# Model dimension counted as 512 a + 4 p + j, expert weights in 8 KB pieces, output weights and weighted sums stored block by block

## The chip, the cores and the metric

The kernel runs on one core of a Trainium2 chip. The metric is the device time of one execution in microseconds (us); lower is better. The engines are called as in the profile: PE (TensorE matmuls), PEld (its weight loads, which overlap the matmuls), DVE (VectorE), ACT (ScalarE), POOL (GpSimd), SP (the queue that issues nearly all loads from HBM).

## The reference

Two layers of a decoder trunk on one sequence of 256 tokens with 1024 features, all in float32. Layer 0 mixes by a causal convolution and stick-breaking attention, layer 1 by gated linear attention and causal pooling; both end with the same mixture of 16 experts, and these carry most of the bytes.

```python
for l in range(DEPTH):                                   # 2
    sh1, sc1, g1, sh2, sc2, g2 = split(silu(c) @ ada_w[l] + ada_b[l], 6)
    h = rmsnorm(x, norm_mix[l]) * (1 + sc1) + sh1
    x = x + g1 * mixer_l(h, w_in, w_out, ...)            # ends in  concat @ w_out
    h = rmsnorm(x, norm_ffn[l]) * (1 + sc2) + sh2
    # 16 experts in 4 groups, top 2 of one group per token
    for e in range(16):
        y += combine[:, e:e+1] * ((silu(h @ w_gate[l, e]) * (h @ w_up[l, e])) @ w_down[l, e])
    x = x + g2 * y
return rmsnorm(x, final_norm)
```

Gate, up and down of one expert are 1024 x 512, 1024 x 512 and 512 x 1024 float32, 2 MB each: 192 MB for both layers.

## The kernel before

**Layout.** The 1024 features lie on 128 partitions in 8 blocks. Feature 256 a + 2 p + j (a below 4, j below 2) is in block 2 a + j on partition p (`rows`, `block`, L72 to L79). A matrix that is contracted over the features is loaded with `rows`, so each partition reads two neighbouring rows. A vector along the features is cut into blocks by `block`, every second element of a run of 256.

**Weights.** All weights pass through one ring of 16 buffers of 1 MB (`buffer`, L50). SP issues their loads in a fixed order, each as soon as the buffer 16 places earlier was read for the last time. `unit` (L62) loads a piece of ada_w (the conditioning products), w_in or w_out; a piece of w_in is two transfers of 512 KB.

**Projections and output products.** `Projections` (w_in) and `Output` (w_out) split each 128 x 512 piece of weight into a high part (ACT, L55) and a low part (DVE, sometimes POOL, L56), and PE multiplies in three passes (L418, L423 and L453). For w_out the weight is PE's stationary operand, and `products` (L453) takes it by `block`, at a step of two elements.

**Experts (`moe`).** Experts are worked in 8 pairs. The two experts of a pair use the two halves of PE's columns. For a pair, `weight` (L1215) loads 12 units of 1 MB: 4 of gate, 4 of up, 4 of down. A unit holds one quarter of the contraction for both experts, so a partition reads 4 KB of each expert. `up` (L1240) takes a unit for every two blocks: 4 matmuls, which the profile shows as 8 records. `act` and `actT` multiply with the SiLU and turn the 512 features onto partitions. `down` (L1277) does the down product, a unit for each of 4 blocks, two halves of 512 columns each. `evicted` and `high_low` (L1305, L1313) weight the result and split it into a high and a low part, and `scatter` (L1330) adds it into the four accumulators: in layer 0 with the parts as stationary operand, taken by `block`; in layer 1 as moving operand. The last pair of layer 0 uses `weighted_parts` (L1321) instead. Ahead of pair 7 stands a branch (`rest`, L1383) that is for experts with more than 64 tokens. In layer 1 the residual is added by 16 transposes that write the accumulators by `block` (L1538).

**Order.** It is written out by hand: pair n + 1's gate and up stand before pair n's down, and what fills the mixers (ada units, splits) is placed by generators.

```python
def rows(w):
    return w.rearrange("(a p j) n -> p a j n", a=4, j=2)
def block(ap, k):
    a, j = k // 2, k % 2
    return ap[:, 256 * a + j:256 * a + 256:2]
```

## Time and profile before

| what | value |
|---|---|
| runs | 791.4, 794.8 and 4035.95 us, median 794.8 |
| profiled execution | 791.18 us |
| its span in the profile | 789.5 us |
| PE busy, share of the span | 730.9 us, 93% |
| loads | 282.46 MB, mean 358 GB/s |
| stages by the timeline | mixer 0 to about 200 us, experts of layer 0 to 425, mixer 1 to 561, experts of layer 1 to 784 |

The profile is of one execution. The span is what its instructions cover; 1.7 us of the execution's own time lie around it. A busy PE is not a PE at its peak, since a matmul's row runs on while the next has begun; so stops and distances between starts say more than busy shares.

### The profile page before, as it was taken

What the parts mean: (1) busy time and instruction counts of PE and PEld (TensorE: products, weight loads), DVE (VectorE), ACT (ScalarE), POOL (GpSimd) and SP (SyncE); (2) the same over time, 40 slices, a digit from 0 to 9 for tenths busy, and PEclk for the clock granted to TensorE, in tenths of its full rate; (3) what the DMA queues carried; (4) which work ended last, traced back from release to release, by engine and by line L of the source; (5) the groups of instructions that cost most, each with busy time, mean ns of one, the idle gap of its engine ahead of it and who ended that gap; (6) DMA issues with size and microseconds to landing.
All of it is one profiled execution on the core that took longest, in us unless ns stands there. A gap on an engine that the chain in (4) does not pass through costs nothing. (4 is left out here: it accounts for less than half of the span.)

```text
span 789.5 us, 10674 instructions
## 1 busy us (share of the span) xinstructions
PE 730.9 (93%) x4173; PEld 402.8 (51%) x4173; DVE 313.8 (40%) x563; ACT 235.1 (30%) x441; POOL 120.0 (15%) x168
## 2 busy tenths in 40 slices
PE   6798888998899999999797999999999999999985
PEld 4398645486434335343233677579534334434323
DVE  3459968675214113121115655453513123213214
ACT  3357657463102101110113544551402101001012
POOL 1357646222000000000004500010300000000000
PEclk9999999999999999999999999999799999999999
DMA  8999739954999999999999998496699999999992
GB/s 357 386 375 419 291 121 398 372 219 183 351 410 409 409 409 409 409 408 409 409 405 391 396 414 322 171 402 235 255 385 412 408 409 409 409 408 409 408 403 106
DMA packets 74713, 282.46 MB, mean 358 GB/s; under 512 B 5194, under 2 KB 6438, under 8 KB 69530
## 3 DMA queue, kind: packets, MB, share of 16 engines
q1 hardware_dynamic: 73122, 278.68, 89.9%
q0 software_dynamic: 1344, 2.64, 0.9%
q8 instruction: 35, 0.57, 0.3%
q10 hardware_dynamic: 184, 0.34, 0.1%
q14 instruction: 28, 0.23, 0.1%
HBM read 280.59 MB, written 1.05 MB: 357 GB/s over the span
## 5 line engine op out<-in xcount | busy, mean ns | idle before, releaser
L1252 PE MATMUL g<-w,xg 128*64 128x512 f32 x512 | 115.0, 597 | 1.9 <-DMA w<-in_moe_w_gate_dram 1.8
L1252 PE MATMUL u<-w,xg 128*64 128x512 f32 x496 | 110.7, 594 | 2.1 <-DMA w<-in_moe_w_up_dram 2.1
L1285 PE MATMUL dn<-w,at 128*64 128x512 f32 x448 | 101.7, 604 | 8.1 <-ACTq L1383 6.8
L1264 DVE TENSOR_TENSOR act<-sg,u 128x512 f32<-128x512 f32 (+1 forms) x18 | 11.1, 628 | 153.0 <-PE u L1252 153.0
L1252 PEld LDWEIGHTS u<-w,xg 128*64 128x64 f32 x496 | 34.6, 137 | 72.1 <-issue 64.7
L1252 PEld LDWEIGHTS g<-w,xg 128*64 128x64 f32 x512 | 35.1, 137 | 68.6 <-issue 61.2
L56 DVE TENSOR_TENSOR g<-wi,g 128x512 fp32r<-128x512 f32 x72 | 58.1, 816 | 24.8 <-ACT g L55 24.6
L1285 PEld LDWEIGHTS dn<-w,at 128*64 128x64 f32 x448 | 31.1, 138 | 70.8 <-issue 56.8
L423 PE MATMUL pj<-hT,g 128*128 128x256 f32 x480 | 61.4, 285 | 6.0 <-DVE g L56 4.7
L423 PEld LDWEIGHTS pj<-hT,g 128*128 128x128 f32 x480 | 57.8, 188 | 10.0 <-DVE g L56 6.8
L418 PE MATMUL pj<-g,hT 128*128 128x512 f32 x192 | 51.3, 414 | 7.4 <-DVE g L56 3.5
L55 ACT ACTIVATE g<-wi 128x512 fp32r<-128x512 f32 x72 | 44.4, 626 | 39.1 <-PE pj L423 20.2
L190 PE MATMUL ada<-ad,cond 128*32 128x512 f32 x384 | 52.0, 653 | 4.0 <-DMA ad<-in_ada_w_dram 4.0
L453 PE MATMUL po<-cat,g 128*128 128x256 f32 x372 | 51.1, 290 | 2.5 <-ACT gsr L1006 1.7
L453 PEld LDWEIGHTS po<-cat,g 128*128 128x128 f32 x372 | 46.8, 196 | 6.7 <-ACT gsr L1006 2.6
L418 PEld LDWEIGHTS pj<-g,hT 128*128 128x128 f32 x192 | 35.4, 193 | 22.4 <-DVE g L56 6.7
L568 POOL TENSOR_TENSOR yc<-yc,cv 128x256 f32<-128x256 f32 x45 | 38.9, 864 | 22.8 <-ACT cv L567 20.0
L553 DVE SCALAR_TENSOR_TENSOR yc<-yp,epar,yc 128x256 f32<-128x256 f32 x56 | 41.3, 737 | 1.0
L1317 ACT ACTIVATE ys<-y 128x512 fp32r<-128x512 f32 x28 | 16.9, 625 | 67.1 <-DVE y L1307 62.3
L1275 DVE COPY at<-at 128x512 f32<-128x512 f32 x14 | 9.7, 692 | 67.5 <-PE at L1274 65.9
L1311 ACT ACTIVATE y<-dn,cw 128x512 f32<-128x512 f32 x7 | 4.8, 687 | 103.8 <-PE dn L1285 103.8
L1260 ACT ACTIVATE sg<-g 128x512 f32<-128x512 f32 x14 | 8.4, 597 | 89.4 <-PE g L1252 89.4
(385 smaller groups left out, 887.4 us busy)
## 6 DMA issues: line engine op xcount, KB each, us to landing
w<-in_moe_w_gate_dram SPq DMA_DIRECT2D x64, 1024.0 KB, 16.1
w<-in_moe_w_up_dram SPq DMA_DIRECT2D x62, 1024.0 KB, 18.3
w<-in_moe_w_down_dram SPq DMA_DIRECT2D x61, 1024.0 KB, 18.3
ad<-in_ada_w_dram SPq DMA_DIRECT2D x48, 1024.0 KB, 8.7
wi<-in_w_in_even_dram SPq DMA_DIRECT2D x20, 512.0 KB, 12.1
wi<-in_w_in_odd_dram SPq DMA_DIRECT2D x14, 512.0 KB, 12.5
wo<-in_w_out_even_dram SPq DMA_DIRECT2D x4, 1024.0 KB
wo<-in_w_out_odd_dram SPq DMA_DIRECT2D x4, 1024.0 KB, 18.6
```

The source lines that it names most:

```text
L55: S.activation(g[0], w, AF.Copy)
L56: (eng or V).tensor_tensor(g[1], w, g[0].bitcast(F32), op=OP.subtract)
L190: PE.matmul(acc[32 * j:32 * j + 32, :], lhsT=cond[:, k, :], rhs=w[:, k - (i if n == 2 else 2 * i), c0:c0 + 512], start=i == 0, stop=i == 4 ...
L418: PE.matmul(bs[t], lhsT=self.h[j][:, k, t * 128:(t + 1) * 128], rhs=g[i], start=k == 0 and p == 0, stop=k == 7 and p == 2)
L423: PE.matmul(bs[c // 2][:, (c % 2) * T:(c % 2 + 1) * T], lhsT=g[i][:, c * 128:(c + 1) * 128], rhs=self.h[j][:, k, :], start=k == 0 and c % ...
L453: PE.matmul(self.acc[kd // 2][:, (kd % 2) * T:(kd % 2 + 1) * T], lhsT=block(g[wi], kd % 4), rhs=cats[ci][:, k, :], start=start and kd % 2 ...
L553: V.scalar_tensor_tensor(yc[:, k], yp[:, k, j:j + T], epar[:, k, j:j + 1], yc[:, k], op0=OP.mult, op1=OP.add)
L568: G.tensor_tensor(y, y, p, op=OP.add)
L1252: PE.matmul(b[64 * e:64 * e + 64, :], lhsT=xg[:, k, o + 64 * e:o + 64 * e + 64], rhs=we[:, e, k % 2 * 512:k % 2 * 512 + 512], start=k == 0 ...
L1264: V.tensor_tensor(a[:, n], sg[:, n], ub[:, n], op=OP.mult)
L1285: PE.matmul(bs[h][64 * e:64 * e + 64, :], lhsT=at[k][:, 64 * e:64 * e + 64], rhs=r[:, e], start=k == 0, stop=k == 3)
L1317: S.activation(ys[:, 0, n], y[h], AF.Copy)
```

## The change

The features are counted as 512 a + 4 p + j, with a below 2 and j below 4, so a partition holds four neighbouring rows. For the experts a unit is now one half of the contraction of one expert: one run of 8 KB per partition, instead of two runs of 4 KB from two experts. PE therefore works on two units at a time, one of each expert. The down weights get the same treatment (two rows per partition), and the transposes of the hidden features follow it with a step of two. Pieces of w_in are one transfer of 1 MB instead of two of 512 KB; pieces of ada_w keep their runs of 8 or 4 KB, from rows four apart instead of two. A step of four elements would now be PE's for w_out and for layer 0's weighted sums; instead ACT, DVE and POOL read at that step while they split, and write block by block, so PE reads contiguous blocks. Other slices by `block` (the transposes of x and of the ada rows, and L1538's writes into PSUM) go from a step of two to four.

```diff
     def unit(name, src, a, eng=SP):
-        if len(src.shape) == 4:
-            for i in range(2):
-                eng.dma_start(t[:, 2 * i:2 * i + 2], src[:, i])
-        else:
-            eng.dma_start(t, src)
+        eng.dma_start(t, src)
...
-        return w.rearrange("(a p j) n -> p a j n", a=4, j=2)
+        return w.rearrange("(a p j) n -> p a j n", a=2, j=4)
...
-        a, j = k // 2, k % 2
-        return ap[:, 256 * a + j:256 * a + 256:2]
+        a, j = k // 4, k % 4
+        return ap[:, 512 * a + j:512 * a + 512:4]
+
+    def by_block(ap):
+        return ap.rearrange("p (q j) -> p j q", j=4)
+
+    def blocks(ap):
+        return ap.rearrange("p (j q) -> p j q", j=4)
...
         def load(self, eng=SP):
-            self.w.append(unit(f"wi{c0}{k}", self.src[:, k // 2:k // 2 + 2, :, c0:c0 + 512], 4, eng))
+            self.w.append(unit(f"wi{c0}{k}", self.src[:, k // 4, :, c0:c0 + 512], 4, eng))
...
         def parts(self, n, half, order, buffers, pool=()):
-                self.g[n][k, q] = split(buffers(i), ws[k // 2][:, k % 2, 512 * q:512 * q + 512], G if i in pool else None)
+                self.g[n][k, q] = buffers(i)
+                split([blocks(g) for g in self.g[n][k, q]], by_block(ws[k // 2][:, k % 2, 512 * q:512 * q + 512]),
+                      G if i in pool else None)
...
         def products(self, n, cats, k, kd, start=False, stop=False):
-                PE.matmul(..., lhsT=block(g[wi], kd % 4),
+                PE.matmul(..., lhsT=g[wi][:, kd % 4 * 128:kd % 4 * 128 + 128],
...
         def weight(pr, i, out=None, eng=SP):
+            e = 2 * pr + i % 2
             if i < 8:
-                src = (moe_w_gate, moe_w_up)[i // 4][l, 2 * pr:2 * pr + 2]
-                src = src.rearrange("e (a p j) n -> p a e (j n)", a=4, j=2)[:, i % 4]
+                src = rows((moe_w_gate, moe_w_up)[i // 4][l, e])[:, i // 2 % 2]
             else:
-                src = moe_w_down[l, 2 * pr:2 * pr + 2, (i - 8) * 128:(i - 7) * 128].rearrange("e p n -> p e n")
+                src = rows_down(e)[:, (i - 8) // 2]
...
+        def rows_down(e):
+            return moe_w_down[l, e].rearrange("(a p j) n -> p a j n", a=2, j=2)
...
         def up(pr, s, w, xg, name, between=None):
-                if k % 2 == 0:
-                    we = next(w)
+                if k % 4 == 0:
+                    we = [next(w), next(w)]
                 for e in range(2):
-                              rhs=we[:, e, k % 2 * 512:k % 2 * 512 + 512], start=k == 0, stop=k == 7)
+                              rhs=we[e][:, k % 4], start=k == 0, stop=k == 7)
...
         def actT(pr, s, a, *at):
-                    PE.transpose(b[:, k, :], a[:, i * n + k, :], ident)
+                    f = i * n + k
+                    PE.transpose(b[:, k, :], a[:, f // 2 * 256 + f % 2:f // 2 * 256 + 256:2], ident)
...
         def down(pr, w, at):
-            for k in range(2 if l and pr == 7 else 4):
-                we = next(w)
-                for h, n in enumerate(cols):
-                    product(h, k, we[:, :, n])
+            for a in range(1 if l and pr == 7 else 2):
+                we = [next(w), next(w)]
+                for j in range(2):
+                    for h, n in enumerate(cols):
+                        product(h, 2 * a + j, [w_[:, j, n] for w_ in we])
...
         def high_low(pr, s, y):
-                S.activation(ys[:, 0, n], y[h], AF.Copy)
-                V.tensor_tensor(ys[:, 1, n], y[h], ys[:, 0, n].bitcast(F32), op=OP.subtract)
+                yh, hi, lo = y[h], ys[:, 0, n], ys[:, 1, n]
+                if l == 0:
+                    yh, hi, lo = by_block(yh), blocks(hi), blocks(lo)
+                S.activation(hi, yh, AF.Copy)
+                V.tensor_tensor(lo, yh, hi.bitcast(F32), op=OP.subtract)
...
         def weighted_parts(pr, s, bs, cw):
+                hi, lo, b = blocks(hi), blocks(lo), by_block(bs[h])
...
         def scatter(ys, pt, n, first=False, last=False):
-                        PE.matmul(..., lhsT=block(ys[i], k),
+                        PE.matmul(..., lhsT=ys[i][:, 128 * k:128 * k + 128],
```

PE at the gate product of pair 7 in layer 0, before: `g0_7_0` is the gate's bank in PSUM, `w0_7_0` to `w0_7_3` are pair 7's gate units, and the number after each is the buffer's.

```order
L1252 MATMUL g0_7_0_2920<-w0_7_0_2921,xg0_3_2684 64x512 x4
L1252 MATMUL g0_7_0_2920<-w0_7_1_2927,xg0_3_2684 64x512 x4
L1252 MATMUL g0_7_0_2920<-w0_7_2_2933,xg0_3_2684 64x512 x4
L1252 MATMUL g0_7_0_2920<-w0_7_3_2939,xg0_3_2684 64x512 x4
```

The same place now (the line is L1260 in the new file):

```order
L1260 MATMUL g0_7_0_2906<-w0_7_0_2907,xg0_3_2670 64x512
L1260 MATMUL g0_7_0_2906<-w0_7_1_2909,xg0_3_2670 64x512
L1260 MATMUL g0_7_0_2906<-w0_7_0_2907,xg0_3_2670 64x512
L1260 MATMUL g0_7_0_2906<-w0_7_1_2909,xg0_3_2670 64x512
L1260 MATMUL g0_7_0_2906<-w0_7_0_2907,xg0_3_2670 64x512
L1260 MATMUL g0_7_0_2906<-w0_7_1_2909,xg0_3_2670 64x512
L1260 MATMUL g0_7_0_2906<-w0_7_0_2907,xg0_3_2670 64x512
L1260 MATMUL g0_7_0_2906<-w0_7_1_2909,xg0_3_2670 64x512
L1260 MATMUL g0_7_0_2906<-w0_7_2_2919,xg0_3_2670 64x512
```

The number of matmuls is the same (16); four of them needed one unit each, now eight alternate between two units, so the second unit's arrival has eight less one matmuls behind it instead of four.

SP at the same place, before: the loads of pair 7's gate and the first of pair 6's down.

```order
L1236 DMA w0_7_0_2921<-in_moe_w_gate_dram 128x2x1024
L1236 DMA w0_7_1_2927<-in_moe_w_gate_dram 128x2x1024
L1236 DMA w0_7_2_2933<-in_moe_w_gate_dram 128x2x1024
L1236 DMA w0_7_3_2939<-in_moe_w_gate_dram 128x2x1024
L1236 DMA w0_6_8_2963<-in_moe_w_down_dram 128x2x1024
```

And now:

```order
L1240 DMA w0_7_0_2907<-in_moe_w_gate_dram 128x2048
L1240 DMA w0_7_1_2909<-in_moe_w_gate_dram 128x2048
L1240 DMA w0_7_2_2919<-in_moe_w_gate_dram 128x2048
L1240 DMA w0_7_3_2921<-in_moe_w_gate_dram 128x2048
L1240 DMA w0_6_8_2949<-in_moe_w_down_dram 128x2048
```

The number and the order of the transfers stay; each partition's share is one run of 2048 elements instead of two of 1024.

## Rows read from the trace of the kernel before

**Rows 1.** The page: busy engines, and DMA in 40 slices.
```profile
PE 730.9 (93%) x4173; PEld 402.8 (51%) x4173; DVE 313.8 (40%) x563; ACT 235.1 (30%) x441; POOL 120.0 (15%) x168
...
DMA  8999739954999999999999998496699999999992
```

**Rows 2.** Busy time by stretch: stretch, its length, engines, clock, DMA share, GB/s.
```profile
60.00:78.00 18.00, 15.64 (x123) 14.62 (x123) 17.86 (x23) 13.80 (x29) 14.10 (x16) 1.00 1.01 420
30.00:50.00 20.00, 18.50 (x140) 16.00 (x133) 12.25 (x23) 13.88 (x26) 11.60 (x14) 1.00 1.06 381
215.00:300.00 85.00, 85.00 (x443) 36.94 (x444) 18.57 (x31) 10.78 (x19) 0.22 (x1) 1.00 1.02 408
300.00:390.00 90.00, 84.72 (x421) 33.40 (x422) 18.05 (x29) 11.27 (x19) 0.00 (x0) 1.00 1.03 409
590.00:700.00 110.00, 110.00 (x550) 47.33 (x550) 26.41 (x44) 13.91 (x24) 0.00 (x0) 1.00 1.03 409
```

**Rows 3.** Tile w, 591 to 754 us: what its engine's idle time waited for.
```profile
  DMA w<-in_moe_w_gate_dram: 0.6, 2
...
  DMA w<-in_moe_w_up_dram: 0.3, 1
  DMA w<-in_moe_w_down_dram: 0.3, 1
```

**Rows 4.** Timeline of PE in layer 1's experts, gates of pairs 2 and 4.
```profile
612.02 7.09 PE L1252 MATMUL g<-w,xg 128*64 128x512 f32 x32
...
663.35 7.09 PE L1252 MATMUL g<-w,xg 128*64 128x512 f32 x32
```

**Rows 5.** Timeline of PE in layer 0's experts: start, length, [idle before it].
```profile
208.75 3.65 PE L1252 MATMUL g<-w,xg 128*64 128x512 f32 x16
...
272.86 7.09 PE L1252 MATMUL g<-w,xg 128*64 128x512 f32 x32
...
324.32 7.09 PE L1252 MATMUL g<-w,xg 128*64 128x512 f32 x32
331.24 3.60 PE L1252 MATMUL u<-w,xg 128*64 128x512 f32 x16
...
381.21 1.94 PE L1252 MATMUL g<-w,xg 128*64 128x512 f32 x8
...
388.79 1.94 PE L1252 MATMUL g<-w,xg 128*64 128x512 f32 x8 [0.62 <-DMA w<-in_moe_w_gate_dram]
390.66 2.21 PE L1335 MATMUL acc<-pt,ys 128*128 128x256 f32 x16
396.15 8.78 PE L1285 MATMUL dn<-w,at 128*64 128x512 f32 x32 [3.28 <-ACTq L1383]
```

**Rows 6.** Timeline of SP's queue as layer 0's experts begin.
```profile
204.72 3.37 SPq L1236 DMA_DIRECT2D w<-in_moe_w_up_dram  x2
210.72 3.96 SPq L1236 DMA_DIRECT2D w<-in_moe_w_down_dram  x4
```

**Rows 7.** Groups by line and form: weight loads, splits, a stepped read and plain ones.
```profile
L453 PE MATMUL po<-cat,g 128*128 128x256 f32 x372 | 51.1, 290 | 2.5 <-ACT gsr L1006 1.7 <-ACT g L55 0.5 <-DVE g L56 0.2
L453 PEld LDWEIGHTS po<-cat,g 128*128 128x128 f32 x372 | 46.8, 196 | 6.7 <-ACT gsr L1006 2.6 <-issue 1.8 <-ACT g L55 1.6
L423 PEld LDWEIGHTS pj<-hT,g 128*128 128x128 f32 x480 | 57.8, 188 | 10.0 <-DVE g L56 6.8 <-DVE hT L329 1.7 <-issue 1.2
L55 ACT ACTIVATE g<-wo 128x512 fp32r<-128x512 f32 x31 | 18.4, 622 | 1.5 <-PE po L453 1.5
L56 DVE TENSOR_TENSOR g<-wo,g 128x512 fp32r<-128x512 f32 x26 | 19.6, 775 | 14.9 <-ACT g L55 14.7
L56 POOL TENSOR_TENSOR g<-wo,g 128x512 fp32r<-128x512 f32 x5 | 6.6, 1312 | 36.1 <-DVE g L56 19.0 <-ACT g L55 13.0 <-ACT rc L380 4.1
L130 DVE COPY vcol<-vcol 128x136 f32<-128x136 f32 x1 | 0.3, 300 | 5.8 <-PE vcol L129 5.8
L1275 DVE COPY at<-at 128x512 f32<-128x512 f32 x14 | 9.7, 692 | 67.5 <-PE at L1274 65.9 <-DMA w<-in_moe_w_down_dram 1.6
L1275 DVE COPY at_7sq<-at 128x256 f32<-128x256 f32 x2 | 0.9, 426 | 1.2 <-PE at L1274 1.2
L1538 PE MATMUL acc<-ident,xT 128*128 128x128 f32 x32 | 3.7, 275 | 0.0
L1274 PE MATMUL at<-ident,act 128*128 128x128 f32 x64 | 10.3, 284 | 0.0
```

More of the change, by code (lines that the diff above doesn't have):

```diff
@@ L233, in small_loads @@
         G.dma_start(rb, router_bias.rearrange("(o e) -> o e", o=1).broadcast_to([128, E]))
-        for a in range(4):
-            G.dma_start(rw[:, 2 * a:2 * a + 2], rows(router_w)[:, a])
-        for a in range(4):
-            G.dma_start(walow[:, 2 * a:2 * a + 2, 0:16], rows(w_in_odd[0])[:, a, :, 1536:1552])
+        for a in range(2):
+            G.dma_start(rw[:, 4 * a:4 * a + 4], rows(router_w)[:, a])
+        for a in range(2):
+            G.dma_start(walow[:, 4 * a:4 * a + 4, 0:16], rows(w_in_odd[0])[:, a, :, 1536:1552])
         for j in range(4):
@@ L1296, in down @@
                     for k in range(2):
-                        product(h, 2 + k, we[:, k, :, within(n)])
+                        product(h, 2 + k, [we[:, k, e, within(n)] for e in range(2)])
             return bs
```

27 lines of the change are left out of this document (13 added, 14 removed).

## The prediction

> **What bounds the kernel now.** I read the page first, then busy time by stretch, then the tile of the expert weights, then PE's and SP's timelines, and the groups by line last. The page shows two engines at their limit: PE is busy for 93% of the span, and the DMA engines stand at 9 tenths or more in most slices [rows 1]. So the first question is which of the two ends last in the two expert stages, since the change touches the loads there. By stretch, the expert weights come at 408 to 409 GB/s in both layers, at a DMA share above 1: the transfers never pause [rows 2]. That alone would make the loads the bound, but a full queue isn't a late one. A unit that lands before PE wants it costs nothing.
>
> In layer 1 PE does not wait. Between 591 and 754 us its engine's stops for expert weights sum to 1.2 us, in four places [rows 3]. From pair 2's gate to pair 4's gate, 612.02 to 663.35, are 51.33 us [rows 4]. In that time PE eats 24 units of 1.0486 MB, 490 GB/s, while 409 GB/s arrive. It lives on the ring that was filled during the mixer, and the stage is over before that is used up. Layer 1's experts are bound by PE.
>
> In layer 0 the ring runs dry. Pair 3's gate starts at 272.86, pair 5's at 324.32 and pair 7's at 381.21 [rows 5]: 51.46 us for two pairs, as in layer 1, then 56.89. Pair 7's gate takes 9.45 us (381.21 to 390.66) where pair 5's took 6.92 (324.32 to 331.24), with stops for gate units. The lag by loads is 5.43 + 2.53 = 7.96 us. That is all that faster loads can give here; after the branch (396.15) PE's next stop is not for weights. Mixers and the start I treat below.
>
> **The change part by part.** The sum is made against the profiled execution, 791.18 us, of which 789.5 are span and 1.7 lie around it.
>
> *Bigger pieces.* The trace has 8 KB pieces already: the units of ada_w that fill 60 to 78 us, at 420 GB/s [rows 2]. A unit of 1.0486 MB takes 2.50 us at that rate and 2.57 at 408.5, 2.7% less. In layer 0 this counts from about 215 us, when the queue is full, to the last gate unit of pair 7 (its matmuls start at 388.79): 173.8 us, so that unit lands 4.8 us earlier. In layer 1 it gives 0, since PE waits for nothing there. The bound from below is 0 (the pieces of the experts come no faster), from above the 7.96 us of lag.
>
> *Ring slots come free in twos.* SP issues new loads as PE gives back buffers, two from 204.72 and four from 210.72 [rows 6]. One gate unit used to come free after each 4 matmuls. Now the first two are read in turn and both come free when the second was free before, near 207.6, and the next two when the group that starts at 208.75 ends, at 212.4 [rows 5]. The third load, issued at 210.72, so comes 1.7 us later and the first 2.9; queued behind it are all further loads, and the stream of layer 0 starts later by that as long as its queue is not full. I take 1.5 us, bounds 0 and 2.9.
>
> *PE works in twos.* Where PE waits for weights, what follows the last landing was one unit's work, 1.87 us (388.79 to 390.66), and is now two units' work, 3.6 us (331.24, 16 records) [rows 5]: 1.7 us later, less one matmul that can go ahead. Queued behind are the scatter, the branch and all of pair 7. Cost 1.7 us, bounds 0 (loads no longer late) and 1.7.
>
> These three are one chain in layer 0: 4.8 - 1.5 - 1.7 = 1.6 us gained. Its bounds are 7.96 gained and 4.6 lost (2.9 + 1.7, if the rate stays). In layer 1 the same two costs meet a PE that isn't waiting: 0.
>
> *Contiguous stationary operands.* The output products load their weights in 196 ns at a step of two, the projections theirs in 188 contiguous [rows 7]. 372 loads by 8 ns are 3.0 us if each were on the path, 0 if the matmuls cover them. Loads overlap matmuls, so I take a quarter, 0.8 us gained. Layer 0's scatter gets the same, but there PE waits for loads anyway: 0.
>
> *Stepped reads on ACT, DVE and POOL.* The 32 splits of w_out (622 ns on ACT, 775 on DVE, 1312 on POOL) and layer 0's 16 high and low parts now read every fourth float. Lower bound 0: the one stepped read of this length in the trace, the copy of vcol from PSUM at a step of 17 floats, took 300 ns for 136 elements. Plain copies took 426 for 256 and 692 for 512, 1.04 ns an element, and so would give 301 [rows 7]. Upper bound: each split takes twice as long. The output products stop for splits for only 0.7 us in all [rows 7], so only splits that stand ahead of a layer's first product count in full, three in layer 0 and two in layer 1: 5 x (0.62 + 0.78) = 7.0 us, and 1.4 at the end of layer 0's experts. The nearest row is the stepped copy, so I take 0.4.
>
> The Trainium skill speaks against this edit: "SBUF — State Buffer", section "Door 1: The DMA port swizzle", says that SBUF is read in lines of 16 bytes, that two hits per line are needed for full rate and that each new line costs something. A step of four floats hits each line once. "GPSIMD Engine Reference", section "Performance pitfalls for Q7 kernels", gives GpSimd about half as much again for steps above 8 bytes; by that the five POOL splits would be an estimated 0.66 us longer each. The trace has no such read from SBUF; what the rule would do is the second rival.
>
> *Steps of four elsewhere.* Transposes of x stand beside the first ada loads. Those of the ada rows and the 32 records of L1538, which write PSUM at a step, are on PE's path. L1538 at a step of two takes 275 ns a record, the contiguous transposes of L1274 284 [rows 7]: the step costs nothing yet. Bounds 0 and 3.7 us (L1538 twice as long); I take 0.4.
>
> *w_in in one transfer.* The first half of a piece can be used only with the second: 512 KB at 381 GB/s, 1.4 us, where PE waits for w_in, which after the start it doesn't. I take 0.3, bounds 0 and 1.4.
>
> Sum: -1.6 - 0.8 + 0.4 + 0.4 + 0.3 = -1.3 us, 789.9, which I round to 790.0. The two ordinary runs shown are 791.4 and 794.8, so a median like the one shown could lie up to 3 us above this for the same kernel.
>
> **The rivals.** 2% of 791.2 is 15.8 us, about what a measurement of this kernel can tell from no change: faster is below 775.4, slower above 807.0.
>
> *The loads bound everything.* For it: DMA at 9 tenths throughout both expert stages. Then all 192 expert units gain 0.07 us: 13.4 us, 777.8. Against it: rows 3 and 4. Even this stays within 2%. Chance 0.08.
>
> *The whole lag of layer 0 goes.* If slots in twos delay nothing, and the faster stream is enough to keep PE fed to pair 7, then 7.96 us go, and with the small terms the time is 783.5. Against it: 4.8 us of gain are less than 7.96 of lag. Chance 0.12.
>
> *The stepped accesses cost double.* Place: splits ahead of the output products, the end of layer 0's experts, L1538. Price 7.0 + 1.4 + 3.7 = 12.1 us, against 2.4 gained: about 801, slower. It decides from 2.4 us on, when stepped accesses take a fifth longer. For it: no row shows such a read from SBUF. Against it: the stepped copy from PSUM at full rate. It is what the rule of lines of 16 bytes would give. Chance 0.14.
>
> *The change doesn't do what it says.* The experts' pieces come no faster than before, say because they are at the rate of HBM and not of the pieces; the twos still cost: 791.2 + 4.6 - 0.8 + 1.1 = 796. Against it: 420 GB/s at 60 to 78 us. Chance 0.10.
>
> **How the numbers follow.** My forecast has 0.56; the likeliest case's own range is 786 to 794. The range of 782 to 800 takes in the second and the last rival and most of the third; it leaves out the first and the far end of the third, about 0.15. Faster by over 2% would need more than all loads can give: 0.04. Slower by over 2% would need stepped accesses at more than double: 0.05. Within 2%: 0.91.
>
> **What would show it.** In the profile after, layer 0's experts should move about 420 GB/s; pair 7's gate should start and end 1 to 3 us earlier, with fewer but longer stops; layer 1's two pairs should take 51.3 us as before. Splits of w_out should keep 0.62 and about 0.7 us. I am wrong if layer 1's experts get shorter by several us, if splits take 0.9 us or more, or if the rate in the experts stays at 409.

## The result, and the profile after

The changed kernel takes 803.86 us (median of 800.65 to 805.37), the kernel before 793.14 beside it; the ratio is 1.0116, with an interval of 1.0078 to 1.0153. So it is slower by about 1.2%, clear of noise, where I forecast 1.3 us less and let the range end at 800. The profiled execution took 804.9 us with a span of 803.2, 13.7 us above before's 789.5. The medians are 10.7 us apart: the profile of before is of a short execution, that of the changed kernel of a longer one.

The page of the changed kernel, its first part and two lines of the second; they answer to [rows 1].

```profile
PE 739.3 (92%) x4173; PEld 409.5 (51%) x4173; DVE 331.2 (41%) x563; ACT 258.6 (32%) x441; POOL 119.5 (15%) x163
...
PEclk9999979988899999999999999999999999999998
DMA  8999639845599999999999998488599999999981
```

ACT is busy for 23.5 us more and DVE for 17.4 us more, with the same number of instructions. The clock stands at 7 or 8 tenths in the slice from 100 to 120 us and in three from 161 to 221, and DMA at 5 from 201 to 221, where it was at 9: layer 0's experts begin later. To place the loss I cut the span at the same five events of PE's timeline in each kernel: the first product of attention scores, the first output product of mixer 0, layer 0's first gate product, the statistics after layer 0's experts, and layer 1's first gate product.

| stretch, us | before | after | difference |
|---|---|---|---|
| start to the scores | 105.83 | 105.44 | -0.4 |
| scores to the first output product | 46.12 | 52.07 | +5.95 |
| to layer 0's first gate product | 50.62 | 58.25 | +7.63 |
| layer 0's experts | 222.57 | 221.28 | -1.3 |
| mixer 1 | 140.02 | 139.14 | -0.9 |
| layer 1's experts and the end | 224.34 | 227.02 | +2.7 |

Mixer 0, from the scores on, loses 13.6 us, which is nearly the whole; the other rows about cancel. The experts of layer 0, for which the change was judged, gain 1.3 us, where I had put 1.6. Here is what PE waits for from the scores to the first gate product, after and then before.

```profile
PE gm L677 <- DVE yc L575: 4.1, 1, 4.1
...
PE po L458 <- ACT g L55: 2.1, 1, 2.1
PE att L666 <- ACT zs L655: 2.0, 1, 2.0
PE po L458 <- DVE cat L755: 1.8, 1, 1.8
PE po L458 <- DVE g L56: 1.1, 2, 0.6
```

```profile
...
PE att L661 <- ACT zs L650: 2.0, 1, 2.0
PE gm L672 <- DVE yc L570: 1.1, 1, 1.1
...
PE po L453 <- ACT g L55: 0.5, 1, 0.5
PE po L453 <- DVE g L56: 0.2, 1, 0.2
```

Each row has the sum, the number of waits and the longest. Four waits grew: for the convolution (`yc`, by 3.0 us), for splits of w_out on ACT (1.6) and DVE (0.9), and for `cat`, the input of the output product (1.8, new). The two stretches of mixer 0 by busy time (stretch, its length, then PE, PEld, DVE, ACT and POOL, each with its number of records, then granted clock, DMA share, GB/s), before and then after:

```profile
105.83:151.95 46.12, 42.99 (x266) 21.08 (x266) 31.86 (x49) 29.93 (x56) 24.46 (x29) 0.93 0.82 320
151.95:202.57 50.62, 46.24 (x349) 38.77 (x348) 31.03 (x67) 24.56 (x44) 9.71 (x8) 0.94 0.64 250
```

```profile
105.44:157.51 52.07, 46.00 (x267) 22.57 (x266) 32.73 (x49) 31.26 (x56) 24.47 (x29) 0.87 0.78 298
157.51:215.76 58.25, 49.60 (x350) 40.38 (x348) 35.34 (x67) 31.64 (x44) 10.88 (x8) 0.87 0.53 201
```

PE stands without work for 14.7 us instead of 7.5, so 7.2 of the 13.6 us are stops. The other 6.4 are the same matmuls taking longer, 95.6 us instead of 89.2, at a mean clock of 0.87 instead of 0.93 to 0.94.

The groups of the changed kernel by line and form say why it stops; they answer to [rows 7] (L458 is L453 of before, L1283 L1274, L1553 L1538).

```profile
L458 PE MATMUL po<-cat,g 128*128 128x256 f32 x372 | 53.6, 299 | 8.1 <-ACT gsr L1011 3.1 <-ACT g L55 2.1 <-DVE cat L755 1.8
L458 PEld LDWEIGHTS po<-cat,g 128*128 128x128 f32 x372 | 48.8, 200 | 13.4 <-ACT gsr L1011 4.0 <-ACT g L55 3.1 <-issue 2.6
L55 ACT ACTIVATE g<-wo 128x512 fp32r<-128x512 f32 x31 | 34.2, 1132 | 0.2
L56 DVE TENSOR_TENSOR g<-wo,g 128x512 fp32r<-128x512 f32 x26 | 28.4, 1111 | 19.4 <-ACT g L55 19.3
L56 POOL TENSOR_TENSOR g<-wo,g 128x512 fp32r<-128x512 f32 x5 | 8.0, 1590 | 44.4 <-ACT g L55 40.4 <-ACT rc L383 4.0
L1342 ACT ACTIVATE ys<-dn,cw 128x512 fp32r<-128x512 f32 x2 | 1.4, 687 | 16.1 <-PE dn L1294 16.1
L1283 PEld LDWEIGHTS at<-ident,act 128*128 128x128 f32 x64 | 9.0, 207 | 11.1 <-issue 10.8 <-PE acc L1455 0.2
L1553 PE MATMUL acc<-ident,xT 128*128 128x128 f32 x32 | 3.7, 275 | 0.0
```

A split of w_out takes 1132 ns on ACT (622 before), 1111 on DVE (775) and 1590 on POOL (1312). ACT has no gap left ahead of its splits (0.2 us in all), and DVE's idle time ahead of its own is for ACT. But L1342, the same step of four read from PSUM, takes 687 ns (688 before), and L1553, which writes PSUM at a step of four, 275 as at a step of two. Layer 0's weighted sums, which are read from SBUF, in the groups of 216 to 440 us:

```profile
L1331 ACT ACTIVATE ys<-y 128x512 fp32r<-128x512 f32 x14 | 15.6, 1146 | 3.3 <-DVE y L1319 3.1
L1332 DVE TENSOR_TENSOR ys<-y,ys 128x512 fp32r<-128x512 f32 x14 | 15.0, 1100 | 0.9 <-ACT ys L1331 0.9
```

They took 624 and 686 ns before, as layer 1's without a step still do (626 and 686). For 512 elements 1100 to 1150 ns are about 2.2 ns each, in both places and on both engines.

From the chain on ACT and DVE to PE's clock: the stretch ahead of the wait for `yc`, in ACT's and then DVE's timeline.

```profile
145.51 2.25 ACT L55 ACTIVATE g<-wo 128x512 fp32r<-128x512 f32 x2
147.67 0.89 ACT L572 ACTIVATE cv<-yp,epar 128x256 f32<-128x256 f32 x2
```

```profile
146.70 2.17 DVE L56 TENSOR_TENSOR g<-wo,g 128x512 fp32r<-128x512 f32 x2 [1.76 <-ACT g L55]
148.78 0.68 DVE L653 TENSOR_TENSOR zs<-zs,zc 128x512 f32<-128x512 f32 x1
149.37 0.42 DVE L654 TENSOR_TENSOR zs<-zs,zc 128x256 f32<-128x256 f32 x1
149.70 1.30 DVE L558 SCALAR_TENSOR_TENSOR yc<-yp,epar,yc 128x256 f32<-128x256 f32 x2
151.11 0.42 DVE L575 TENSOR_TENSOR yc<-yc,more 128x256 f32<-128x256 f32 x1
```

Two splits stand in both queues ahead of the last taps of the convolution, and PE's group norm (`gm`) waits for those, not for the weights. Before, the two splits took 1.13 us on ACT and 1.29 on DVE. (Not all of the 3.0 us are theirs, as the runs below show.) The output product needs them only at 157.51. Here is busy time by stretch after, over four stretches of mixer 0, and then before over the whole of its output products but the first.

```profile
107.80:119.10 11.30, 11.30 (x51) 4.95 (x50) 5.46 (x7) 6.77 (x10) 4.56 (x6) 0.55 0.29 99
151.70:155.10 3.40, 3.40 (x14) 1.24 (x18) 0.75 (x2) 1.01 (x2) 0.00 (x0) 0.60 0.85 357
168.60:172.00 3.40, 3.40 (x19) 3.40 (x20) 2.59 (x4) 3.37 (x4) 0.00 (x0) 0.62 0.01 2
179.60:186.50 6.90, 5.55 (x23) 3.55 (x23) 5.51 (x8) 4.19 (x7) 3.60 (x3) 0.51 0.39 137
```

```profile
155.30:189.00 33.70, 32.87 (x269) 30.22 (x268) 19.14 (x34) 15.80 (x30) 4.61 (x4) 1.00 0.59 231
```

After each of the longer stops PE goes on at a clock of 0.51 to 0.62, mostly the lower of its two levels, 1.2 GHz; before, the output products ran at 1.00. So a stop can be paid twice, as itself and as matmuls that take up to twice as long behind it. Not every stop is: PE stops 2.0 us for `zs` (the attention's part from ACT) in both kernels, and goes on at 0.62 before (137.4 to 140.3 us) and at 1.00 after (140.0 to 143.0). The stretch from 107.8 lies ahead of the first split of w_out; the runs below tell where it and the one from 151.7 belong.

The experts of layer 0 in PE's timeline answer to [rows 5].

```profile
286.83 7.09 PE L1260 MATMUL g<-w,xg 128*64 128x512 f32 x32
...
338.41 7.09 PE L1260 MATMUL g<-w,xg 128*64 128x512 f32 x32
...
393.46 4.50 PE L1260 MATMUL g<-w,xg 128*64 128x512 f32 x18
399.15 3.65 PE L1260 MATMUL g<-w,xg 128*64 128x512 f32 x14 [1.19 <-DMA w<-in_moe_w_gate_dram]
402.73 2.16 PE L1350 MATMUL acc<-pt,ys 128*128 128x256 f32 x16
405.45 4.48 PE L1294 MATMUL dn<-w,at 128*64 128x512 f32 x18 [0.56 <-PEq L1398]
410.26 3.22 PE L1294 MATMUL dn<-w,at 128*64 128x512 f32 x13 [0.34 <-DMA w<-in_moe_w_down_dram]
...
415.44 3.65 PE L1260 MATMUL u<-w,xg 128*64 128x512 f32 x14 [1.52 <-DMA w<-in_moe_w_up_dram]
```

Two pairs take 51.58 us, then 55.05, and pair 7's gate 9.27: a lag of 3.47 + 2.35 = 5.8 us instead of 7.96. One long stop has taken the place of three short ones. The branch costs 0.56 us now instead of 3.28, but the down and up units behind it are late by 0.34 and 1.52.

### The profile page after: what moved, and what is told of

Same layout as the page of the kernel before. It is cut to its first block, busy times and chain, and to the rows that moved or that the text cites. A ratio compares the mean times of both kernels' runs of the same rounds, so it can differ in the third digit from the quotient of the medians.

```text
span 803.2 us, 10622 instructions
## 1 busy us (share of the span) xinstructions
PE 739.3 (92%) x4173; PEld 409.5 (51%) x4173; DVE 331.2 (41%) x563; ACT 258.6 (32%) x441; POOL 119.5 (15%) x163
## 5 line engine op out<-in xcount | busy, mean ns | idle before, releaser
L1260 PE MATMUL g<-w,xg 128*64 128x512 f32 x512 | 115.9, 599 | 2.1 <-DMA w<-in_moe_w_gate_dram 1.2
L1260 PE MATMUL u<-w,xg 128*64 128x512 f32 x496 | 112.9, 594 | 1.5 <-DMA w<-in_moe_w_up_dram 1.5
L1294 PE MATMUL dn<-w,at 128*64 128x512 f32 x448 | 103.5, 604 | 4.4 <-ACTq L1398 3.5
L1260 PEld LDWEIGHTS u<-w,xg 128*64 128x64 f32 x496 | 36.9, 137 | 70.9 <-issue 64.8
L1260 PEld LDWEIGHTS g<-w,xg 128*64 128x64 f32 x512 | 36.3, 137 | 68.2 <-issue 60.7
L426 PEld LDWEIGHTS pj<-hT,g 128*128 128x128 f32 x480 | 57.7, 188 | 10.7 <-DVE g L56 6.9
L458 PE MATMUL po<-cat,g 128*128 128x256 f32 x372 | 53.6, 299 | 8.1 <-ACT gsr L1011 3.1
L193 PE MATMUL ada<-ad,cond 128*32 128x512 f32 x384 | 53.7, 673 | 4.6 <-DMA ad<-in_ada_w_dram 4.6
L458 PEld LDWEIGHTS po<-cat,g 128*128 128x128 f32 x372 | 48.8, 200 | 13.4 <-ACT gsr L1011 4.0
L1331 ACT ACTIVATE ys<-y 128x512 fp32r<-128x512 f32 x28 | 24.1, 886 | 67.4 <-DVE y L1317 64.2
L56 DVE TENSOR_TENSOR g<-wo,g 128x512 fp32r<-128x512 f32 x26 | 28.4, 1111 | 19.4 <-ACT g L55 19.3
## 6 DMA issues: line engine op xcount, KB each, us to landing
wo<-in_w_out_even_dram SPq DMA_DIRECT2D x4, 1024.0 KB, 12.8
wo<-in_w_out_odd_dram SPq DMA_DIRECT2D x4, 1024.0 KB, 17.5
```

The source lines that it names most:

```text
L56: (eng or V).tensor_tensor(g[1], w, g[0].bitcast(F32), op=OP.subtract)
L193: PE.matmul(acc[32 * j:32 * j + 32, :], lhsT=cond[:, k, :], rhs=w[:, k - (i if n == 2 else 2 * i), c0:c0 + 512], start=i == 0, stop=i == 4 ...
L426: PE.matmul(bs[c // 2][:, (c % 2) * T:(c % 2 + 1) * T], lhsT=g[i][:, c * 128:(c + 1) * 128], rhs=self.h[j][:, k, :], start=k == 0 and c % ...
L458: PE.matmul(self.acc[kd // 2][:, (kd % 2) * T:(kd % 2 + 1) * T], lhsT=g[wi][:, kd % 4 * 128:kd % 4 * 128 + 128], rhs=cats[ci][:, k, :], st ...
L1260: PE.matmul(b[64 * e:64 * e + 64, :], lhsT=xg[:, k, o + 64 * e:o + 64 * e + 64], rhs=we[e][:, k % 4], start=k == 0, stop=k == 7)
L1294: PE.matmul(bs[h][64 * e:64 * e + 64, :], lhsT=at[k][:, 64 * e:64 * e + 64], rhs=r[e], start=k == 0, stop=k == 3)
```

## The experiments

Two theories stood against each other first: A, the step of four on ACT and DVE holds up mixer 0; B, mixer 0 is late for its clock from 107.8 us on or for the pieces of w_in and ada_w. Each run is timed beside the kernel before on the same chip, and the ratios are to that.

| kernel | us | ratio, interval | scores to first gate product | layer 0's experts |
|---|---|---|---|---|
| before | | | 96.74 | 222.57 |
| changed | 803.86 | 1.0116 (1.0078 to 1.0153) | 110.32 | 221.28 |
| changed, again | 803.92 | 1.0106 (1.0041 to 1.0172) | 108.80 | 221.60 |
| steps on PE | 839.89 | 1.0556 (1.0471 to 1.0642) | 118.86 | 225.20 |
| w_out's steps on PE | 835.64 | 1.0499 (1.0416 to 1.0583) | 118.64 | 221.25 |
| steps in the writes | 804.15 | 1.0130 (1.0091 to 1.0168) | 105.21 | 222.54 |
| 4 KB pieces | 807.77 | 1.0156 (1.0074 to 1.0239) | 107.08 | 223.40 |
| two steps of two | 792.98 | 0.9985 (0.9954 to 1.0016) | 99.83 | 220.92 |
| same, plain transposes | 791.80 | 0.9974 (0.9947 to 1.0001) | 97.33 | 220.55 |
| that one again | 793.73 | 0.9971 (0.9946 to 0.9997) | 100.52 | 220.97 |
| that one, 4 KB pieces | 794.28 | 0.9981 (0.9957 to 1.0005) | 98.30 | 223.99 |
| that one, by expert | 838.54 | 1.0538 (1.0502 to 1.0573) | 101.84 | 239.87 |
| ACT's steps alone | 796.60 | 1.0018 (0.9990 to 1.0045) | 102.31 | 221.43 |
| no steps | 973.95 | other routing | 97.62 | |

**All steps back on PE.**

```diff
-                split([blocks(g) for g in self.g[n][k, q]], by_block(ws[k // 2][:, k % 2, 512 * q:512 * q + 512]),
-                      G if i in pool else None)
+                split(self.g[n][k, q], ws[k // 2][:, k % 2, 512 * q:512 * q + 512], G if i in pool else None)
...
-                PE.matmul(..., lhsT=g[wi][:, kd % 4 * 128:kd % 4 * 128 + 128],
+                PE.matmul(..., lhsT=block(g[wi], kd % 4),
...
-                    yh, hi, lo = by_block(yh), blocks(hi), blocks(lo)
...
-                hi, lo, b = blocks(hi), blocks(lo), by_block(bs[h])
+                b = bs[h]
...
-                        PE.matmul(..., lhsT=ys[i][:, 128 * k:128 * k + 128],
+                        PE.matmul(..., lhsT=block(ys[i], k),
```

> The changed kernel with all splits plain again: ACT, DVE and POOL read and write contiguously, and PE takes w_out and layer 0's weighted sums as stationary operand at a step of four elements. Theory A (stepped reads on ACT and DVE hold up mixer 0): a w_out split on ACT goes from 1132 ns back to 622, on DVE from 1111 to 775; the first gate product of layer 0 starts near 203 us instead of 215.8; the time is 789 to 793 us, a ratio to the kernel before of 0.995 to 1.002. Theory B (mixer 0 is later for the clock at 108 to 119 us, ahead of the first w_out split, or for the pieces of w_in and ada_w): the first gate product stays past 211 us and the time at 800 us or more, ratio 1.01. If PE pays for the step of four instead, the w_out weight load is well above the 196 ns that it took at a step of two.

The splits were back at 623 and 732 ns, and yet the kernel took 840 us. The third outcome named in the expectation had come, and far stronger than I had thought. Two groups of this run:

```profile
L457 PE MATMUL po<-cat,g 128*128 128x256 f32 x372 | 92.2, 404 | 1.7 <-ACT gsr L1010 1.7
L457 PEld LDWEIGHTS po<-cat,g 128*128 128x128 f32 x372 | 88.8, 330 | 5.0 <-ACT gsr L1010 2.6 <-issue 1.3 <-ACT g L55 0.8
```

A weight load that took 196 ns at a step of two and 189 contiguous (the run without steps) takes 330 at a step of four, and matmuls no longer cover it: the output products of mixer 0 and 1 grew by about 20 us each. So sorting on ACT and DVE is not an extra of this change: for this order of features, it is the cheaper of two payments.

**Only w_out's steps on PE.** The first two edits of that diff, to the splits and the products of w_out, without the rest.

> The changed kernel with only the splits of w_out plain again (PE reads w_out at a step of four); layer 0's weighted sums keep their stepped splits. Theory A, with the loss in the mixers alone: within 1 us of the kernel with all splits plain, 789 to 793 us. If the stepped high and low parts of the weighted sums (886 and 893 ns, were 625 and 685) hold up PE at the end of layer 0's experts, this kernel is 1 to 1.5 us above that one. Theory B: 800 us or more.

835.6 us: theory A, as I had it (the cost is ACT's and DVE's alone), had failed in its number again, for the same reason. The comparison I wanted it for still holds: with the weighted sums' steps on ACT and DVE layer 0's experts take 221.25 us, with those on PE 225.20. In that stage the moved steps are hidden.

**Read in order, write at a step.** The splits take the elements in the order in which they lie and write them 512 bytes apart.

```diff
+    def natural(ap):
+        return ap.rearrange("p (q j) -> p q j", j=4)
+
+    def stepped_out(ap):
+        return ap.rearrange("p (j q) -> p q j", j=4)
...
-                split([blocks(g) for g in self.g[n][k, q]], by_block(ws[k // 2][:, k % 2, 512 * q:512 * q + 512]),
+                split([stepped_out(g) for g in self.g[n][k, q]], natural(ws[k // 2][:, k % 2, 512 * q:512 * q + 512]),
...
-                    yh, hi, lo = by_block(yh), blocks(hi), blocks(lo)
+                    yh, hi, lo = natural(yh), stepped_out(hi), stepped_out(lo)
...
-                hi, lo, b = blocks(hi), blocks(lo), by_block(bs[h])
+                hi, lo, b = stepped_out(hi), stepped_out(lo), natural(bs[h])
```

> The changed kernel with the same splits in the other order: source read contiguously, result written at 512-byte distances, so PE still reads contiguous blocks. If what costs is the read at a step of 16 bytes, a w_out split is back at 620 to 700 ns on ACT and 780 to 900 on DVE, and the time is 789 to 794 us. If a step costs the same on either side, ACT stays near 1132 ns and the time at 800 to 806 us.

1146 ns on ACT, 1173 on DVE, 1800 on POOL, and 804 us: it doesn't matter on which side the step is. The last weighted sums of layer 0 tell the two memories apart. There ACT reads PSUM and writes SBUF: with the step on the read it takes 687 ns (L1342 above), with the step on the write 1120 here.

**Two steps of two.** Features four apart are two steps of two: ACT, DVE and POOL sort even from odd, and PE takes every second of a half.

```diff
-        return ap.rearrange("p (q j) -> p j q", j=4)
+        return ap.rearrange("p (q j) -> p j q", j=2)
...
-        return ap.rearrange("p (j q) -> p j q", j=4)
+        return ap.rearrange("p (j q) -> p j q", j=2)
+
+    def half_block(ap, j):
+        return ap[:, j % 2 * 256 + j // 2:j % 2 * 256 + 256:2]
...
-                PE.matmul(..., lhsT=g[wi][:, kd % 4 * 128:kd % 4 * 128 + 128],
+                PE.matmul(..., lhsT=half_block(g[wi], kd % 4),
...
-                        PE.matmul(..., lhsT=ys[i][:, 128 * k:128 * k + 128],
+                        PE.matmul(..., lhsT=half_block(ys[i][:, k // 4 * 512:k // 4 * 512 + 512], k % 4),
```

> The changed kernel with the step of four done in two steps of two: ACT, DVE and POOL read at a step of two floats and write two half blocks, and PE takes its block at a step of two from them. Theory A (a step of 16 bytes is what costs, 8 bytes nearly nothing): a w_out split takes 620 to 650 ns on ACT and 690 to 800 on DVE, a w_out weight load 196 ns, and the time is 788 to 793 us, 11 to 15 below the changed kernel. Rival C (any step halves the engines' rate): ACT stays at 1100 ns or more and the time at 803 us or more. Theory B of the first runs (the loss is in the clock or in w_in) expects 800 or more too, with short splits.

The layout is the same and so is the number of instructions; the time falls to 793 us, where a run of the changed kernel beside it took 803.9. Its groups:

```profile
L461 PEld LDWEIGHTS po<-cat,g 128*128 128x128 f32 x372 | 46.8, 196 | 7.2 <-ACT gsr L1014 2.7 <-issue 1.8 <-ACT g L55 1.7
L55 ACT ACTIVATE g<-wo 128x512 fp32r<-128x512 f32 x31 | 19.9, 672 | 1.4 <-PE po L461 1.2
L56 DVE TENSOR_TENSOR g<-wo,g 128x512 fp32r<-128x512 f32 x26 | 19.7, 774 | 15.5 <-ACT g L55 15.2
L56 POOL TENSOR_TENSOR g<-wo,g 128x512 fp32r<-128x512 f32 x5 | 7.0, 1401 | 36.9 <-ACT g L55 32.7 <-ACT rc L386 4.2
```

A step of 8 bytes costs ACT 50 ns (672, above the 620 to 650 expected), POOL 89, DVE nothing and PE 8. Rival C (any step halves the rate) is out, and theory A holds in this form: for the splits and for w_out's weight loads a step of 16 bytes in SBUF is dear, one of 8 nearly free. PE's transposes of plain float32 do not fit it: their weight loads take 140 ns contiguous, but 207 at 8 bytes (hidden features) and 208 at 16 (the ada rows). The Trainium skill has the rule in "SBUF — State Buffer", section "Door 1: The DMA port swizzle": lines of 16 bytes, two hits per line for full rate. The splits agree: 672 ns on ACT with two hits a line, 1132 with one. The passage goes on that "how far you can stride for free depends on dtype: 4 fp32"; here a step of four float32 is not free, and the measurement decides. It also says that PSUM has lines of 8 bytes and that any pattern there that is not contiguous slows matmuls much; L1553's writes at a step, 275 ns at 8 and at 16 bytes, do not show that.

**With plain transposes as well.** The product with the SiLU reads at a step of two, so that PE transposes contiguous blocks.

```diff
-                V.tensor_tensor(a[:, n], sg[:, n], ub[:, n], op=OP.mult)
...
+                o = o.rearrange("s (a j p) -> s a j p", j=2, p=128)
+                x, y = (t.rearrange("s (a p j) -> s a j p", j=2, p=128) for t in (x, y))
+                V.tensor_tensor(o, x, y, op=OP.mult)
...
-                    PE.transpose(b[:, k, :], a[:, f // 2 * 256 + f % 2:f // 2 * 256 + 256:2], ident)
+                    PE.transpose(b[:, k, :], a[:, i * n + k, :], ident)
```

> As the kernel with two steps of two, and the product with the SiLU (DVE) reads its factors at a step of two and writes contiguous blocks, so the 14 groups of transposes of the hidden features are contiguous on PE. A group of four transposes went from 0.66 to 0.74 us with the change, and its followers from 0.42 to 0.50 later: 14 x 0.08 to 0.1 = 1.1 to 1.4 us less than the kernel with two steps, if the product stays at 628 ns on DVE; no gain, or a loss of some tenths a pair, if it gets longer and holds up the transposes.

The transposes' weight loads went from 207 ns back to 140, and the product stayed at 687. 1.2 us less by the medians, 0.4 us of it in layer 0's experts; the intervals overlap, so the gain is not shown by the times alone.

**No steps.** Contiguous splits and contiguous blocks, so the output features aren't sorted at all.

> The changed kernel with contiguous splits and contiguous blocks on PE: the sorting of the output features is left out (of w_out and of layer 0's weighted sums), so the features are added in another order than the reference's and routing differs; the amount of work is the same. The price of the steps alone, with no step anywhere in its place. Theory A: first gate product of layer 0 at 200 to 203 us, time 788 to 792 us. Theory B: 800 or more.

Routing changed so that the branch for large experts ran, and the total says nothing. The part ahead of routing does: the first gate product comes at 202.50 us, 97.62 after the scores, where the changed kernel takes 110.32 and 108.80. That is 11 to 13 us between single profiles; the next run tells how much of it is chance.

**The changed kernel again.**

> The changed kernel again, to see what moves without an edit: 800 to 806 us. If the stretch at half the clock from 108 to 119 us was chance, it begins or ends elsewhere here and the mixer stage moves by up to 3 us; if it belongs to the change, it is there again.

803.9 us. PE's clock over the stretch from 107.8 to 119.1 in this run, in the kernel with two steps and in that with plain transposes; the three are alike up to there:

```profile
107.80:119.10 11.30, 11.30 (x57) 5.05 (x58) 5.37 (x7) 6.66 (x10) 4.87 (x6) 0.70 0.42 145
```

```profile
107.80:119.10 11.30, 11.30 (x51) 5.24 (x52) 5.47 (x7) 6.77 (x10) 4.40 (x6) 0.57 0.29 97
```

```profile
107.80:119.10 11.30, 11.30 (x68) 5.97 (x67) 5.78 (x8) 6.71 (x11) 5.29 (x7) 0.85 0.38 128
```

0.70, 0.57 and 0.85, where the changed kernel's first profile had 0.55 and before 0.85. The clock in this stretch varies from run to run whatever the kernel. From the first score to the first product of `zc`, where the stretch ends, the first profile takes 13.67 us and before 10.65, but the kernel with two steps takes 13.56 and that with plain transposes 10.60: 3 of the 13.6 us of mixer 0 in the first profile are chance.

The stretch from 151.7 is not the steps' alone either. It is there in this run, but in two other profiles with all steps of four (steps in the writes, and the changed kernel with 4 KB pieces, below) the clock falls behind the stop for `zs` instead, at 138 to 143 us, as in before. PE then reaches its group norm some 1.6 us later and waits that much less for `yc`. The wait in the changed kernel with 4 KB pieces, where the clock fell there, and in the kernel with two steps and 4 KB pieces, where it did not:

```profile
150.29 1.10 PE L677 MATMUL gm<-yc,bones 128*128 128x512 f32 x2 [2.41 <-DVE yc L575]
```

```profile
149.66 1.10 PE L680 MATMUL gm<-yc,bones 128*128 128x512 f32 x2 [2.76 <-DVE yc L578]
```

Like with like, the splits add 1.3 us to this wait (2.41 against before's 1.13, 4.07 against 2.76), and not the 3.0 that the first two profiles showed.

The later two stretches do belong to the steps. All four profiles with steps of four on ACT and DVE (both of the changed kernel, steps in the writes, 4 KB pieces) have a lower clock between 162 and 173 us and again between 175 and 187. In before, the five with two steps, no steps and ACT's steps alone it is 1.00 from 155 to 170 and from 176 to 188; only the second run of two steps with plain transposes and the run by expert (both below) have a short stretch at 0.57, near 171 to 175.5, with no stop ahead of it.

Mixer 0 is the same code in several of these kernels, so all profiles together tell the price better than two:

| profiles | scores to first gate product, us | PE without work | PE busy | granted clock |
|---|---|---|---|---|
| before | 96.74 | 7.5 | 89.2 | 0.93 |
| no steps | 97.62 | 7.7 | 90.0 | 0.92 |
| two steps of two, five profiles | 97.33 to 101.84, mean 99.6 | 7.9 to 9.5 | 88.9 to 92.3 | 0.90 to 0.94 |
| ACT's steps alone | 102.31 | 9.3 | 93.1 | 0.90 |
| steps in the writes | 105.21 | 12.8 | 92.4 | 0.90 |
| changed, three profiles | 107.08 to 110.32, mean 108.7 | 12.3 to 14.7 | 94.1 to 95.6 | 0.87 to 0.88 |

Against two steps of two, the steps of four cost mixer 0 about 9 us, half of it in stops and half in longer matmuls; profiles of the same mixer differ by up to 4.5. In the whole time it is 10.9 (803.9 against 793.0). The kernels with two steps load w_in and ada_w as the changed kernel does, so of theory B only the 3 us of chance are left.

**4 KB pieces,** once in the changed kernel, once in that with two steps and plain transposes: a unit holds two 4 KB runs of two experts, PE takes one unit at a time.

```diff
-            e = 2 * pr + i % 2
+            k = i % 4
             if i < 8:
-                src = rows((moe_w_gate, moe_w_up)[i // 4][l, e])[:, i // 2 % 2]
+                src = (moe_w_gate, moe_w_up)[i // 4][l, 2 * pr:2 * pr + 2]
+                src = src.rearrange("e (a p j) n -> p a e j n", a=2, j=4)[:, k // 2, :, k % 2 * 2:k % 2 * 2 + 2].rearrange("p e j n -> p e (j n)")
...
-                if k % 4 == 0:
-                    we = [next(w), next(w)]
+                if k % 2 == 0:
+                    we = next(w)
...
```

> The changed kernel with expert units of two 4 KB runs from two experts again (same order of features, same splits, same transposes), so a unit is enough for four matmuls and ring buffers come free one by one. Layer 0's experts took 222.6 us before and 221.3 after, from the first gate product to the statistics. If bigger pieces gain 4.8 us and working in twos gives back 3.2, as predicted, they take about 222.9 here, and the time is 1 to 2.5 us above the changed kernel's, 804 to 806 us. If the piece's size makes no difference, the time is 1 to 3 us below it, 800 to 802. Transfers come at 408 GB/s instead of 421.

> The kernel with two steps of two and contiguous transposes, with expert units of two 4 KB runs from two experts instead of one of 8 KB: the price of the pieces without the steps. With the 2.0 us that layer 0's experts differed by between the changed kernel (221.3) and the one with 4 KB pieces (223.4), they take about 222.5 here instead of 220.6, at 408 instead of 421 GB/s, and the time is 793 to 795 us. If the pieces' gain needs the late start of the changed kernel, the difference is under 1 us and the time 791 to 792.5.

Layer 0's experts take 2.1 or 1.8 us more in the first (223.40 for 221.28 and 221.60) and 3.4 or 3.0 in the second (223.99 for 220.55 and 220.97). A stretch of them in the second, and the same stretch in the kernel with 8 KB:

```profile
220.00:300.00 80.00, 80.00 (x410) 32.96 (x407) 15.72 (x28) 8.63 (x14) 0.00 (x0) 1.00 1.03 410
```

```profile
220.00:300.00 80.00, 80.00 (x415) 34.15 (x412) 16.98 (x29) 9.72 (x16) 0.00 (x0) 1.00 1.01 422
```

410 GB/s against 422. The pieces do what I said of them, and net of the twos a little more. In the whole time the first takes 807.8 us, above the 804 to 806 expected, but its ratio's interval takes in the changed kernel's; the second pair of kernels differs by 0.1% of ratio only, with overlapping intervals.

**Expert by expert.** Does it have to be in twos?

```diff
         def up(pr, s, w, xg, name, between=None):
...
+            if not between:
+                for k in range(0, 8, 4):
+                    for e in range(2):
+                        we = next(w)
+                        for i in range(k, k + 4):
+                            PE.matmul(b[64 * e:64 * e + 64, :], lhsT=xg[:, i, o + 64 * e:o + 64 * e + 64],
+                                      rhs=we[:, i % 4], start=i == 0, stop=i == 7)
+                return b
...
         def down(pr, w, at):
...
-                we = [next(w), next(w)]
-                for j in range(2):
-                    for h, n in enumerate(cols):
-                        product(h, 2 * a + j, [w_[:, j, n] for w_ in we])
+                for e in range(2):
+                    w_ = next(w)
+                    for j in range(2):
+                        for h, n in enumerate(cols):
+                            product(h, 2 * a + j, [w_[:, j, n]] * 2, [e])
```

> The kernel with two steps of two and contiguous transposes, and PE takes the units of a pair one after the other: in gate, up and down all products of one expert with its 8 KB unit, then those of the other (but for the gate of a layer's first pair). So a unit is enough to begin, and its buffer comes free when its four products are done. If working in twos costs what the prediction put (1.5 for the buffers, of which the first pair's share stays, and 1.7 for the last landing), layer 0's experts take 217.5 to 219.5 us instead of 220.6 and the time is 1 to 3 us less, 788.5 to 791. Rival: the two experts' products run beside each other in the two halves of PE's columns only when they alternate; then a gate takes well over 6.92 us, up to twice that, the experts of both layers tens of us more, and the time is over 830.

The rival came true. A down product in PE's timeline:

```profile
654.66 8.97 PE L1306 MATMUL dn<-w,at 128*64 128x512 f32 x32
```

8.97 us for 32 records instead of 7.09, and the kernel takes 45 to 47 us more than the one that it was made from (838.5 against 793.7 and 791.8). So the two experts' products are faster when they alternate between the two halves of the columns, by a fifth. The Trainium skill's "TensorEngine Tiling (Array Packing)", section "Performance Considerations", gives 2x column tiling for a stationary operand of 64 columns. Whether it is the products that overlap in the two halves, or the weight loads that hide better, no run here separates. Working in twos is the price of 8 KB pieces here, with one expert to a unit.

**ACT's steps alone.**

```diff
+                hi, lo = self.g[n][k, q]
+                S.activation(blocks(hi), by_block(ws[k // 2][:, k % 2, 512 * q:512 * q + 512]), AF.Copy)
+                (G if i in pool else V).tensor_tensor(lo, hi.bitcast(F32), hi.bitcast(F32), op=OP.subtract)
```

> The changed kernel with the stepped split of w_out on ACT alone: DVE and POOL subtract the high part from itself, contiguous and of the same size, so the low part of w_out is left out (it is zero). If ACT's 1132 ns are what mixer 0 waits for, DVE is back at 700 to 780 ns and yet the first gate product of layer 0 stays at 211 to 215 us, time 799 to 804. If DVE's 1111 ns are, it moves to 203 to 207 us, time 791 to 795. If both in turn (the low part follows the high part in the same chain), it lies between, at 207 to 211.

DVE went to 692 ns (83 less than a plain split; both its sources are the same tile here), POOL to 1042 (1312), and ACT stayed at 1130. The first gate product came at 207.70, between the two cases, but only 0.7 us past the bound of the second, and two profiles of one kernel differ by more. PE's waits say it better. It stops for ACT's splits as long as in the changed kernel (2.1 us, 0.5 before), for `yc` 2.0 (2.4 where DVE's and POOL's steps stand too, 1.1 before, at the same clock ahead of it) and for `cat` 0.5 (1.3 to 1.8). ACT's steps bring part of the stops, DVE's and POOL's the rest: both in turn.

By the ratios (two steps 0.9985, this 1.0018, changed 1.0116), ACT's steps alone cost about 0.3% and DVE's and POOL's on top of them about 1%, 2.6 and 7.8 us. The first is within the noise, since the intervals overlap, and since DVE and POOL run faster here than in a plain split it comes out too small and the second too large. That the second is the larger fits the queues (the low part follows the high part, and DVE carries the convolution and the group norm too), but is not shown. In the changed kernel mixer 1, with 15 such splits on ACT, lost nothing (139.1 us, 140.0 before).

**The best version again.** Two steps of two with plain transposes.

> The kernel with two steps of two and contiguous transposes again, for a narrower interval: 790.5 to 793 us. If it beats the kernel before as layer 0's experts say (220.6 instead of 222.6 us), the ratio is 0.996 to 0.998; if the split's 672 ns on ACT (622 before) give it back, 0.999 to 1.001.

0.9971 (0.9946 to 0.9997), as expected, though its 793.7 us lie just above the 790.5 to 793 expected: faster than before by 0.3%, which the interval barely shows and that of its first run (up to 1.0001) does not, and clearly faster than the changed kernel.

## Why the prediction was wrong, step by step

- **What bounds the kernel** was right. Layer 1's two pairs take 51.47 us (51.33 before), and the loads at 421 GB/s change nothing there.
- **Bigger pieces, ring slots and twos** were right in sum: 1.6 us put; the lag fell by 2.1, the stage by 1.3 and 1.0 in the changed kernel's two profiles, and by 1.8 to 3.4 against 4 KB pieces in the same layout. Their parts (4.8 gained, 1.5 and 1.7 lost) weren't separated.
- **Contiguous stationary operands** went as said (layer 0's scatter 195 to 188 ns, the output products 196 to 189 in the run without steps), but no gain shows: without any step mixer 0 takes 97.62 us from the scores, 96.74 before.
- **Stepped reads on ACT, DVE and POOL** is the step that failed, "so I take 0.4": the steps of four cost about 9 us in mixer 0 and 10.9 in all. Two things were wrong in it. The size: I took the nearest row, a copy out of PSUM, for a read out of SBUF. PSUM reads at a step are free (687 ns at the end of layer 0); SBUF's cost 1.8, 1.4 and 1.2 times on ACT, DVE and POOL (0.28 us a split on POOL, where the estimate was 0.66). A split of 0.9 us or more was one of my own signs of being wrong. The Trainium skill's rule stood beside it and I gave it 0.14. The place: "only splits that stand ahead of a layer's first product count in full". It took the stops of before for a measure of slack, while the splits stand in queues that also carry the convolution. In mixer 0, 16 splits on ACT are 17.5 us instead of 9.3, and 13 on DVE 14.3 instead of 10.8. PE stops for `yc`, `cat` and the splits, some 5 us more than with two steps, and its clock falls behind the later of these stops, which costs about as much again; the forecast had no term for the clock.
- **The rival with doubled steps** had the right sign and nearly the right time (801), in part by luck. It charged the five splits ahead of the first products, L1553 and the end of layer 0's experts. The latter two cost nothing, and what it left out, `yc`, `cat` and the clock, made up for them. I had also written that about 2% is what a measurement can tell here; the intervals tell 1.2% apart.
- **Steps of four elsewhere, w_in in one transfer:** nothing lost (275 ns a record; the scores start 0.4 us earlier). What I missed is the step of two at the transposes of the hidden features: 140 to 207 ns a weight load, 0.08 us a group.
- **Layer 1's end**: 2.7 us longer. 1.7 of it is a down product at the lower clock from 766 us on, behind the branch; such a stretch is in both runs of the changed kernel and also in the first run of the best version (752 to 756), but not in its second, though PE stops 3.3 to 3.7 us at the branch in each, and 3.5 before. Whether the change brings it stays open.

## What to carry to other kernels

A new order of data must be priced at every operand that is read against it, per engine and per memory: a step of two floats in SBUF was nearly free here for the splits and w_out's weight loads (not for PE's transposes, 140 to 207 ns), four floats cost ACT, DVE and PE each 40 to 80% of the instruction, and four can be split into two steps of two on two engines. Stops in the trace of before are no measure of the slack of an engine that will become slower; ask for the sum of its added time in one queue, and what else stands in that queue (the same splits cost mixer 1 nothing). A stretch compared between two single profiles can mislead by some us, as the 3.0 us of `yc` did. And where a row for an operation is lacking, a row from another memory is not the nearest one.

## What the hardware showed that I had not expected

- A stationary operand at a step of 16 bytes: 330 ns a load instead of 188, and it no longer hides behind matmuls (in the run with all steps on PE). But the transposes of the ada rows kept 208 ns at a step of four (207 at two); that difference stays unexplained.
- Reads at 16 bytes from PSUM by ACT and DVE: no cost (687 and 751 ns, 688 and 751 before); the same instructions reading in order and writing SBUF at a step of 512 bytes took 1120 and 1108.
- Of the granted clock behind a stop: after the same stop of 2.0 us it fell to between 0.5 and 0.7 for 4 us in the best version's first run and stayed at 1.00 in its second.
